# A hybrid transformer block on one core: sine tables in smaller steps, modulation columns in four steps, weight splits behind the squares at the first exit, and the latents' products two units abreast

## The chip, the core and the metric

The kernel runs on one core of a Trainium2 chip. The metric is the time of one execution on the device in microseconds (us). A core has a matrix engine (PE, with its weight loads, PEld, shown apart), three engines for elementwise work (DVE, ACT, POOL) and an engine that only issues DMAs here (SP). Each engine runs its instructions in the order in which the program queued them; an instruction that waits holds up all those behind it on its engine. POOL issues some of the DMAs too.

## The reference, cut to what matters

One layer, 512 tokens of width 1024, all in float32. The modulation vectors come from one vector `c`, each norm is followed by a scale and a shift, and two feed-forward networks stand around a mixer of two kinds of attention.

```python
mod = silu(c) @ w_ada + b_ada          # 9 x 1024: a shift, a scale and a gate for each part
sh1, s1, g1, sh2, s2, g2, sh3, s3, g3 = split(mod, 9)
h = rms(x) * (1 + s1) + sh1
x = x + 0.5 * g1 * swiglu(h, ffn1_w_in, ffn1_w_out)
h = rms(x) * (1 + s2) + sh2
x = x + g2 * mixer(h, cos(positions * freq), sin(positions * freq))   # gated delta rule and latent attention
h = rms(x) * (1 + s3) + sh3
x = x + 0.5 * g3 * swiglu(h, ffn2_w_in, ffn2_w_out)
```

The latent attention starts with low-rank products of `h` (384 columns of `w_in` for the queries, 256 for keys and values). Its rotary parts need the cosine and the sine of position times frequency.

## The kernel before, in words

**Layout and products.** `x` is held transposed: eight tiles `xT` of 128 features by 512 tokens. Every large product is done in three matmuls (`mm3`, L270 to 274, and its copy L899 to 901): each operand is split in a high part and a low rest (`wh`, `wl` of a weight tile `wr`; `hh`, `hl` of `h`; `ah`, `al` of the activations), and high x high, high x low and low x high are summed in PSUM (`pa`, `pb`). A weight unit is a tile of 1024 x 128 (or a part of it) that SP loads, ACT casts to `wh` and DVE subtracts to `wl`. In `split_w` (L202 to 206) there is another way for the low part: ACT negates the high part into `wl` (L205), and a DMA issued by POOL adds `wr` to it (L206). `plan_units` (L239) lists the units of the mixer and says which of them go that way; `prefetch` (L262) takes the next from the list.

**Stages.** `phase0` transposes and norms `x` and forms the first modulation vectors. `ffn1` runs the first feed-forward network: `enter1` (L903), then a grid of pairs in `ffn_pairs`, whose tasks have fixed steps, then `close` and `leave1` (L1113), which is called the first exit here. `mixer` begins with `latents` (L1320). After the mixer comes `ffn2`, with `leave2` at its end.

**The side work.** While the first feed-forward network keeps PE at work, a `Side` (L52) is advanced step by step; each step runs one generator to its next `yield`. Its generators are
- `ada` (L558): the modulation vectors of the later parts. For each of the 112 tiles of `w_ada` that they need, POOL issues a load (`ar`, L575) some tiles ahead, and DVE multiplies it by a column of silu(c) and adds it to `aa` (L584, L586). When the columns of a group are done, `ada_columns` (L599) sums `aa` over the partitions on PE (L605), copies the sum from PSUM on DVE (`rw`, L608), turns it by PE transposes (L612) and adds the bias on DVE (L616).
- `mixer_consts` (L1160): it loads the small constants of the mixer, transposes the convolution's weights (L1183, copy L1185), and forms angles, sines and cosines. `sincos` (L1253) is a row of small DVE passes on 128 x 128 tiles: a range reduction in two rounds (L1275) and two polynomials (L1285, L1291).

What a step of the side work queues stands, on each engine, between what the feed-forward queues before and after it. In the last pairs a step runs in three of seven program steps, and behind `stop` twice in each.

**A pair's activation.** In `pair_tasks` (L774) the gate's and up's products collect in PSUM (`pb`, L899 to 901); ACT copies a finished one to `cc` (L842), DVE adds (L851), ACT takes the SiLU (L852), DVE multiplies (L861), ACT and DVE split into `ah` and `al` (L863, L867), which the down products read (L272 to 274).

**The first exit.** The last six of the 22 feed-forward blocks of 128 are multiplied by `w_out` in units of their own (`unit_hi`, `unit_lo`, the `wl` of L1049). For the feature tiles 4 to 7, `leave1` does it in two halves of 256 tokens. After each tile DVE adds the product to `xT` (L975, `finish`), and `square_in` (L480) squares it on ACT (L488) and adds the square to `na`: for the first half on POOL (L490), else on DVE. `norm_half` (L492) then sums `na` over the partitions on PE (`colsum`, L548), turns the reciprocal root into a matrix `rb` that all partitions hold, and modulates: `hm` and `hl` on DVE, `hh` on ACT (L459 to 477). Of the weights of the first latents' units, one is asked for behind tile 4 and two behind tile 6 of the second half (`prefetch`).

**The latents.** `first_units` (L502) multiplies three units of `w_in` for the first half of tokens while that half's `h` is being made, then for the second half. `lead` units go abreast, feature tile by feature tile as `h` comes; the others follow one by one. The marks say after which of these steps the second half's norm goes on a step. A unit is asked for behind the first half, its ACT passes behind the last square.

Of the kernel before, what the change touches and what calls it, by code (L numbers as in the profile page):

```python
# [19 lines left out]
NT = 512  # L20
# [69 lines left out]
class Block:  # L90
# [148 lines left out]
    def plan_units(self):  # L239
# [10 lines left out]
        for c in (2056, 2184, 2312, 2440):  # L250
            cols(w, c, True)
# [10 lines left out]
    def prefetch(self, n):  # L262
        while len(self.ready) < n and self.specs:
            self.ready.append(self.specs.pop(0)())

# [193 lines left out]
    def modulate(self, kts, ts, rb, scale, shift, kept=None):  # L459
# [10 lines left out]
        for kt in kts:  # L470
# [3 lines left out]
            nc.scalar.activation(self.h[kt][0][:, ts], t, AF.Identity, bias=shift[:, kt:kt + 1])  # L474
# [5 lines left out]
    def square_in(self, t, ts, acc):  # L480
# [8 lines left out]
        eng = nc.gpsimd if w < NT and ts.start == 0 else nc.vector  # L489
# [12 lines left out]
    def first_units(self, n, nb, lead, marks):  # L502
# [11 lines left out]
        with self.matmuls_in_order(self.last_mm):  # L514
# [16 lines left out]
            with self.traced() as block:  # L531
                self.prefetch(1)
            for x in block:
                if x.engine == mybir.EngineType.Activation:
                    self.follow(x, self.squared)
# [63 lines left out]
    def ada_columns(self, c0, accs):  # L599
# [4 lines left out]
        for q, a in enumerate(accs):  # L604
            nc.tensor.matmul(pr[32 * q:32 * q + 32, :], self.ones[:, :32], a, start=True, stop=True,  # L605
                             tile_position=(0, 32 * q))
        rw = self.slot(s="rw")
        nc.vector.tensor_copy(rw[:32 * n, :], pr[:32 * n, :])  # L608
        yield
        pt = self.aux()  # L610
        for s in range(4):
            nc.tensor.transpose(pt[:, s * P:s * P + 32 * n], rw[:32 * n, s * P:(s + 1) * P], self.ident[:32 * n, :32 * n])  # L612
        col = self.const([P, 4 * n], s="mod")
# [28 lines left out]
    def ffn1(self):  # L642
# [6 lines left out]
        side.add(self.ada(((0, 1), (2, 3, 4, 5), (6, 7, 8, 9), (10, 11)), lambda i: 6 if i < 60 else 3, early=64), self.mixer_consts())  # L649
# [253 lines left out]
    def enter1(self, raws, split, products, glu, tick, side, w1):  # L903

        unit = lambda i: self.unit_split(raws, split, i)
        step = (side.step, 3)
# [20 lines left out]
    def ffn_pairs(self, w1, w2, gate, plain, raws, split, accs, side=None):  # L927
# [185 lines left out]
        def leave1():  # L1113
            accum = self.accum
            side.add(self.ada(((12, 13),), lambda i: 8))
            side.step()
            halves = [slice(0, HALF), slice(HALF, NT)]
            with self.matmuls_in_order(self.ends[mybir.EngineType.PE]):
                for half, ts in enumerate(halves):
                    for t in range(4, KT):  # L1120
# [5 lines left out]
                        self.square_in(t, ts, accum)  # L1126
                        if half and t in (4, 6):
                            self.prefetch(t // 2 - 1)
# [4 lines left out]
                self.prefetch(3)  # L1133
# [26 lines left out]
    def mixer_consts(self):  # L1160
# [19 lines left out]
        for _ in range(6):  # L1180
            yield
# [25 lines left out]
        for nm, gain, sc in (("q", self.gqr, 192.0 ** -0.5), ("k", self.gkr, 1.0)):  # L1207
            both = self.slot(s="rope").rearrange("p (e b c) -> p e b c", e=2, b=NB)
            c, s = both[:, 0], both[:, 1]
            for j in range(2):  # L1210
# [5 lines left out]
                                               op0=ALU.mult, op1=ALU.mult)  # L1216
            self.rope_c[nm], self.rope_s[nm] = c, s
# [35 lines left out]
    def sincos(self, ang):  # L1253
# [12 lines left out]
        for _ in range(2):  # L1266
# [7 lines left out]
            for src, c in ((kh, 0), (kl, 0), (kh, 1), (kl, 1), (kh, 2), (kl, 2), (kh, 3)):  # L1274
                v.scalar_tensor_tensor(out=r, in0=src, scalar=-cs[c], in1=r, op0=ALU.mult, op1=ALU.add)  # L1275
        yield
# [7 lines left out]
        for n in (11, 9, 7, 5, 3):  # L1284
            v.scalar_tensor_tensor(out=sn, in0=sn, scalar=(-1.0 if (n // 2) % 2 else 1.0) / f(n), in1=z, op0=ALU.add,  # L1285
                                   op1=ALU.mult)
# [952 lines left out]
```

## Time and profile before

| what | value |
|---|---|
| time, median of 3 runs | 1067.85 us (1066.84 to 1069.74) |
| time of the profiled execution | 1070.11 us |
| its span in the profile | 1068.4 us |
| mean granted clock of PE | 0.987 of full |
| busy: PE, PEld, DVE, ACT, POOL | 97%, 84%, 71%, 45%, 11% of the span |
| moved by DMA | 140.74 MB, 132 GB/s on the mean |

The stages as they lie in the span: the first feed-forward network to about 400 us with the first exit at its end, the latents from there on, the rest of the mixer and the second feed-forward network behind them.

How it is read: the profile gives busy times, and for each instruction what it waited for. A group or row reads engine, line, operation, output<-input by the program's names, shape. In rows in order of time, the start comes first, then the duration, and a wait ahead of it stands at the end in brackets with the work that ended it. In busy times by stretch, each stretch has its length, then PE, PEld, DVE, ACT and POOL with the number of instructions, then the clock granted to PE, then the DMA engines' share and GB/s. A matmul's duration overlaps that of the next one; the spacing of the starts tells what one costs.

### The profile page before, as it was taken

The page shows a single profiled execution, that of the slowest core. Times are in us where ns is not written, and L with a number is a line of the kernel's source. Part 1 is how long each engine was busy: PE and PEld are TensorE (multiplying, and loading weights), DVE is VectorE, ACT ScalarE, POOL GpSimd, SP SyncE. Part 2 cuts the span into 40 slices and gives each one's busy share as a digit, 9 for nine tenths or more (in the row PEclk, how much of TensorE's full clock was granted, in tenths as well). Part 3 has the DMA queues.
Part 4 walks back from the last instruction along what each step waited for, and adds up shares of the span by engine and source line. Part 5 has one row for each costly group of instructions (what it writes and reads, how often), then busy time and mean ns, then how long its engine had stood idle before and what let it go on. Part 6 is the DMA issues. An engine that isn't in the chain of part 4 may idle for free. (4 is left out here: it accounts for less than half of the span.)

```text
span 1068.4 us, 17063 instructions
## 1 busy us (share of the span) xinstructions
PE 1034.6 (97%) x6659; PEld 897.7 (84%) x6659; DVE 756.2 (71%) x1411; ACT 484.7 (45%) x865; POOL 117.6 (11%) x237
## 2 busy tenths in 40 slices
PE   6999999999999897999999999999999999999998
PEld 4787887888998786987877778988899999999997
DVE  4476888778785764857885765769767787777642
ACT  4342232255554252547747554465434444444332
POOL 0032222121101213100001021220000000000000
PEclk9999999999999997999999999999999999999999
DMA  9995876677664459622121211163432333233222
GB/s 272 280 279 173 273 237 207 191 206 191 177 168 110 124 133 231 159 60 54 48 78 35 77 34 40 41 130 90 137 99 80 119 119 98 81 119 99 65 75 79
DMA packets 187422, 140.74 MB, mean 132 GB/s; under 512 B 14401, under 2 KB 176206, under 8 KB 187342
## 3 DMA queue, kind: packets, MB, share of 16 engines
q1 hardware_dynamic: 175646, 100.33, 33.0%
q0 software_dynamic: 11696, 39.33, 13.5%
q8 instruction: 52, 0.85, 0.3%
q14 instruction: 28, 0.23, 0.1%
HBM read 127.18 MB, written 2.49 MB: 121 GB/s over the span
## 5 line engine op out<-in xcount | busy, mean ns | idle before, releaser
L272 PE MATMUL pa<-ah,wh 128*128 128x512 f32 (+1 forms) x346 | 134.6, 389 | 0.1
L273 PE MATMUL pa<-al,wh 128*128 128x512 f32 (+1 forms) x346 | 133.9, 387 | 0.0
L274 PE MATMUL pa<-ah,wl 128*128 128x512 f32 (+1 forms) x346 | 132.3, 382 | 0.5 <-DVE wl L1049 0.5
L272 PE MATMUL pa<-hh,wh 128*128 128x512 f32 (+1 forms) x293 | 110.7, 378 | 2.2 <-ACT hh L474 2.1
L273 PE MATMUL pa<-hl,wh 128*128 128x512 f32 (+1 forms) x293 | 109.8, 375 | 1.3 <-DVE hl L466 0.9
L274 PE MATMUL pa<-hh,wl 128*128 128x512 f32 (+1 forms) x293 | 108.7, 371 | 0.0
L575 POOL DMA_DIRECT2D ar<-in_w_ada x112 | 63.6, 589 | 174.9 <-DVE aa L586 60.8
L975 DVE SCALAR_TENSOR_TENSOR xT<-pa,mod,xT 128x512 f32<-128x512 f32 (+1 forms) x79 | 57.3, 728 | 35.0 <-PE pa L274 34.7
L274 PEld LDWEIGHTS pa<-ah,wl 128*128 128x128 f32 x346 | 66.1, 191 | 13.9 <-DVE wl L1049 0.9
L586 DVE SCALAR_TENSOR_TENSOR aa<-ar,sc,aa 128x512 f32<-128x512 f32 x98 | 73.2, 747 | 1.3
L272 PEld LDWEIGHTS pa<-ah,wh 128*128 128x128 f32 x346 | 66.9, 193 | 6.7 <-ACT ah L863 0.6
L273 PEld LDWEIGHTS pa<-al,wh 128*128 128x128 f32 x346 | 66.9, 193 | 5.9 <-DVE al L867 0.4
L272 PEld LDWEIGHTS pa<-hh,wh 128*128 128x128 f32 x293 | 55.5, 189 | 14.9 <-ACT hh L474 3.4
L899 PE MATMUL pb<-fh,wh 128*128 128x256 f32 x224 | 63.7, 285 | 0.9 <-ACT cc L842 0.8
L274 PEld LDWEIGHTS pa<-hh,wl 128*128 128x128 f32 x293 | 55.6, 190 | 10.5 <-issue 1.4
L273 PEld LDWEIGHTS pa<-hl,wh 128*128 128x128 f32 x293 | 55.5, 190 | 10.5 <-DVE hl L466 2.6
L901 PE MATMUL pb<-hh,wl 128*128 128x256 f32 x224 | 63.4, 283 | 0.0
L901 PE MATMUL pb<-fh,wl 128*128 128x256 f32 x224 | 63.3, 282 | 0.0
L900 PE MATMUL pb<-fl,wh 128*128 128x256 f32 x224 | 63.2, 282 | 0.0
L900 PE MATMUL pb<-hl,wh 128*128 128x256 f32 x224 | 63.2, 282 | 0.0
L899 PE MATMUL pb<-hh,wh 128*128 128x256 f32 x224 | 63.2, 282 | 0.0
L272 PE MATMUL pb<-hh,wh 128*128 128x512 f32 x149 | 58.6, 393 | 0.0
(448 smaller groups left out, 2789.4 us busy)
## 6 DMA issues: line engine op xcount, KB each, us to landing
wr<-in_ffn_w_in SPq DMA_DIRECT2D x82, 512.0 KB, 3.9
ar<-in_w_ada POOLq DMA_DIRECT2D x112, 256.0 KB, 4.8
wr<-in_ffn_w_out SPq DMA_DIRECT2D x32, 512.0 KB, 3.9
wr<-in_w_in SPq DMA_DIRECT2D x21, 512.0 KB, 3.9
wl<-wr POOLq DMA_DIRECT2D x19, 512.0 KB, 5.5
ar<-in_w_ada SPq DMA_DIRECT2D x16, 512.0 KB, 8.1
wr<-in_ffn_w_out SPq DMA_DIRECT2D x16, 384.0 KB, 3.7
wr<-in_w_out SPq DMA_DIRECT2D x8, 512.0 KB, 3.4
```

The lines of the kernel that those rows point to most:

```text
L272: mm(out, wh, xh, start=start, stop=False)
L273: mm(out, wh, xl, start=False, stop=False)
L274: mm(out, wl, xh, start=False, stop=stop)
L575: nc.gpsimd.dma_start(tiles[i], a1[kc * P:(kc + 1) * P, o:o + NT])
L586: nc.vector.scalar_tensor_tensor(out=acc, in0=a, scalar=sc, in1=acc, op0=ALU.mult, op1=ALU.add)
L899: mm(out, wh, xh, start=start and k == 0, stop=False, **kw)
L900: mm(out, wh, xl, start=False, stop=False, **kw)
L901: mm(out, wl, xh, start=False, stop=stop and k == 3, **kw)
L975: nc.vector.scalar_tensor_tensor(out=self.xT[t][:, ts], in0=p[:, ts], scalar=gate()[:, t:t + 1], in1=self.xT[t][:, ts], op0=ALU.mult, op1= ...
```

## The change

It has five parts; what the kernel computes stays as it was.

1. `ada_columns` yields in three more places, so the column sums, the copy, the transposes and the bias are queued in four steps. `enter1` advances the side work by four steps in place of three at each of its places; 68 of `ada`'s tiles in place of 64 come from the early pool.
2. `mixer_consts` yields four times in place of six ahead of the transpose of the convolution's weights, and within its loop over the rotary tables; `sincos` yields within its loops.
3. At the first exit the first half's squares are added on DVE (`pool=False`). The units' prefetch moves from the second half into the first: one unit behind tile 4, up to three behind tile 7, each with its ACT passes made to follow the last square so far (`prefetch_after`). The first unit gets its low part by a DVE subtraction, the others by ACT and DMA as before.
4. `first_units` runs two units abreast in place of one, and the unit asked for between the halves has its ACT passes behind the last `hh` of the modulation.
5. The last two column groups of `ada` (12 and 13) are started in `latents`, ahead of `first_units`, and not at the head of `leave1`.

```diff
-            cols(w, c, True)
+            cols(w, c, c > 2056)
...
+    def prefetch_after(self, n, name=None):
+        with self.traced() as block:
+            self.prefetch(n)
+        for x in block:
+            if x.engine == mybir.EngineType.Activation:
+                self.follow(x, name or self.squared)
...
-        eng = nc.gpsimd if w < NT and ts.start == 0 else nc.vector
+        eng = nc.gpsimd if pool and w < NT and ts.start == 0 else nc.vector
...
     def ada_columns(self, c0, accs):
...
+        yield
         rw = self.slot(s="rw")
         nc.vector.tensor_copy(rw[:32 * n, :], pr[:32 * n, :])
+        yield
         yield
         pt = self.aux()
...
+        yield
         col = self.const([P, 4 * n], s="mod")
...
-        step = (side.step, 3)
+        step = (side.step, 4)
...
         def leave1():
             accum = self.accum
-            side.add(self.ada(((12, 13),), lambda i: 8))
-            side.step()
...
-                        self.square_in(t, ts, accum)
-                        if half and t in (4, 6):
-                            self.prefetch(t // 2 - 1)
+                        self.square_in(t, ts, accum, False)
+                        if not half and t in (4, KT - 1):
+                            self.prefetch_after(1 if t == 4 else 3)
...
-                self.prefetch(3)
...
-        for _ in range(6):
+        for _ in range(4):
             yield
...
-            for src, c in ((kh, 0), (kl, 0), (kh, 1), (kl, 1), (kh, 2), (kl, 2), (kh, 3)):
+            for i, (src, c) in enumerate(((kh, 0), (kl, 0), (kh, 1), (kl, 1), (kh, 2), (kl, 2), (kh, 3))):
                 v.scalar_tensor_tensor(out=r, in0=src, scalar=-cs[c], in1=r, op0=ALU.mult, op1=ALU.add)
-        yield
+                if i in (2, 4, 6):
+                    yield
...
-        ps = self.first_units(3, nb, 1, (7, 15, 14))
+        self.side.add(self.ada(((12, 13),), lambda i: 8))
+        self.side.step()
+        ps = self.first_units(3, nb, 2, (7, 15, 14), self.modulated)
```

In the polynomials of `sincos` the yields stand after the terms 9 and 5 of the sine and 10, 6 and 2 of the cosine.

Three places show what moves. Lines are those of each kernel's own code (the changed one's run up to 16 lines higher), and the number behind a name tells tiles of one name apart.

On DVE, at the first column group (`aa` of the ada tiles, `rw` the copy of the sums, `mod` the finished columns), before:

```order
L772 TENSOR_TENSOR fl_937<-tv_918,fh_936 128x512
L989 TENSOR_TENSOR wl_859<-wr_857,wh_858 128x1024
L586 SCALAR_TENSOR_TENSOR aa_931<-ar_895,sc_124,aa_931 128x512
L586 SCALAR_TENSOR_TENSOR aa_931<-ar_898,sc_124,aa_931 128x512
L608 COPY rw_978<-pb_975 64x512
L586 SCALAR_TENSOR_TENSOR aa_931<-ar_901,sc_124,aa_931 128x512
L616 TENSOR_TENSOR mod_998<-pb_993,vT_126 128x4x2
```

The same place in the changed kernel:

```order
L590 SCALAR_TENSOR_TENSOR aa_906<-ar_863,sc_124,aa_906 128x512
L613 COPY rw_950<-pb_919 64x512
L590 SCALAR_TENSOR_TENSOR aa_906<-ar_866,sc_124,aa_906 128x512
L694 TENSOR_TENSOR wl_934<-wr_826,wh_933 128x1024
L590 SCALAR_TENSOR_TENSOR aa_906<-ar_908,sc_124,aa_906 128x512
L779 TENSOR_TENSOR fl_957<-tv_937,fh_956 128x512
L996 TENSOR_TENSOR wl_871<-wr_869,wh_870 128x1024
L590 SCALAR_TENSOR_TENSOR aa_906<-ar_911,sc_124,aa_906 128x512
L623 TENSOR_TENSOR mod_985<-pb_969,vT_126 128x4x2
```

The copy of the sums has moved ahead of `fl` and `wl`, and three products lie between it and the bias, where there was one.

On DVE, near the end of the sine block (`sr`, `sz`, `sk`, `skl` are its tiles, `uc` a pair's sum for the SiLU, `wl` a weight's low part), before:

```order
L1275 SCALAR_TENSOR_TENSOR sr_3508<-skh_3512,sr_3508 128x128
L1049 TENSOR_TENSOR wl_3522<-wr_3347,wh_3521 128x768
L1278 TENSOR_SCALAR sr_3508<-sr_3508 128x128
L1279 TENSOR_TENSOR sz_3583<-sr_3508 128x128
L1283 TENSOR_SCALAR sk_3510<-sz_3583 128x128
L1285 SCALAR_TENSOR_TENSOR sk_3510<-sk_3510,sz_3583 128x128 x5
L1287 SCALAR_TENSOR_TENSOR sk_3510<-sk_3510,sr_3508 128x128
L851 TENSOR_TENSOR uc_3305<-uc_3305,pb_3202 128x256
```

In the changed kernel:

```order
L1056 TENSOR_TENSOR wl_3534<-wr_3362,wh_3533 128x768
L1280 SCALAR_TENSOR_TENSOR sr_3468<-skl_3471,sr_3468 128x128
L1280 SCALAR_TENSOR_TENSOR sr_3468<-skh_3472,sr_3468 128x128
L1284 TENSOR_SCALAR sr_3468<-sr_3468 128x128
L1285 TENSOR_TENSOR sz_3583<-sr_3468 128x128
L858 TENSOR_TENSOR uc_3320<-uc_3320,pb_3215 128x256
L1289 TENSOR_SCALAR sk_3470<-sz_3583 128x128
L1291 SCALAR_TENSOR_TENSOR sk_3470<-sk_3470,sz_3583 128x128 x4
```

The pair's sum now stands ahead of the sine's polynomial and not behind it, and the weight's low part stands within the reduction.

On ACT, at the first exit (`sq` the squares, `wh` and `wl` the splits of the latents' units, `rb` the norm's spread), before:

```order
L488 ACTIVATE sq_3782<-xT_106 128x512
L488 ACTIVATE sq_3786<-xT_106 128x512
L203 CAST wh_3936<-wr_3935 128x1024
L205 ACTIVATE wl_3937<-wr_3935 128x1024
L203 CAST wh_4009<-wr_4008 128x1024
L205 ACTIVATE wl_4010<-wr_4008 128x1024
L203 CAST wh_4062<-wr_4061 128x1024
L205 ACTIVATE wl_4063<-wr_4061 128x1024
L488 ACTIVATE sq_3825<-xT_106 128x256
L488 ACTIVATE sq_3848<-xT_106 128x256
L488 ACTIVATE sq_3871<-xT_106 128x256
L488 ACTIVATE sq_3894<-xT_106 128x256
```

In the changed kernel:

```order
L496 ACTIVATE sq_3782<-xT_106 128x512
L496 ACTIVATE sq_3786<-xT_106 128x512
L496 ACTIVATE sq_3809<-xT_106 128x256
L203 CAST wh_3813<-wr_3812 128x1024
L496 ACTIVATE sq_3838<-xT_106 128x256
L496 ACTIVATE sq_3861<-xT_106 128x256
L496 ACTIVATE sq_3884<-xT_106 128x256
L203 CAST wh_3888<-wr_3887 128x1024
L205 ACTIVATE wl_3889<-wr_3887 128x1024
L203 CAST wh_3895<-wr_3894 128x1024
L205 ACTIVATE wl_3896<-wr_3894 128x1024
```

Of six passes that stood ahead of the four squares of the first half, one cast now stands among them and four behind them.

More of the change, by code (lines that the diff above doesn't have):

```diff
@@ L473, in modulate @@
                                            op0=ALU.mult, op1=ALU.mult)
-            nc.scalar.activation(self.h[kt][0][:, ts], t, AF.Identity, bias=shift[:, kt:kt + 1])
+            self.modulated = nc.scalar.activation(self.h[kt][0][:, ts], t, AF.Identity, bias=shift[:, kt:kt + 1]).ins.name
             if last:
@@ L478, in modulate, with square_in @@
         low(*last)
-    def square_in(self, t, ts, acc):
+    def square_in(self, t, ts, acc, pool=True):
         nc = self.nc
@@ L500, in norm_half, with first_units @@
             yield
-    def first_units(self, n, nb, lead, marks):
+    def first_units(self, n, nb, lead, marks, before=None):
         units = [self.next_unit(ahead=0) for _ in range(n)]
@@ L530, in first_units @@
             drain(nb)
[L531 to L535, printed above, removed]
+            self.prefetch_after(1, before)
             ts = slice(HALF, NT)
@@ L648, in ffn1 @@
         side = self.side = Side()
-        side.add(self.ada(((0, 1), (2, 3, 4, 5), (6, 7, 8, 9), (10, 11)), lambda i: 6 if i < 60 else 3, early=64), self.mixer_consts())
+        side.add(self.ada(((0, 1), (2, 3, 4, 5), (6, 7, 8, 9), (10, 11)), lambda i: 6 if i < 60 else 3, early=68), self.mixer_consts())
         def tail():
@@ L1273, in sincos @@
             yield
-            for src, c in ((kh, 0), (kl, 0), (kh, 1), (kl, 1), (kh, 2), (kl, 2), (kh, 3)):
+            for i, (src, c) in enumerate(((kh, 0), (kl, 0), (kh, 1), (kl, 1), (kh, 2), (kl, 2), (kh, 3))):
                 v.scalar_tensor_tensor(out=r, in0=src, scalar=-cs[c], in1=r, op0=ALU.mult, op1=ALU.add)
-        yield
+                if i in (2, 4, 6):
+                    yield
         z = self.slot(s="sz")[:, :P]
@@ L1286, in sincos @@
                                    op1=ALU.mult)
+            if n in (9, 5):
+                yield
         v.scalar_tensor_tensor(out=sn, in0=sn, scalar=1.0, in1=r, op0=ALU.add, op1=ALU.mult)
@@ L1292, in sincos @@
                                    op1=ALU.mult)
+            if n in (10, 6, 2):
+                yield
         v.tensor_scalar(out=cn, in0=cn, scalar1=1.0, scalar2=None, op0=ALU.add)
```

## The prediction

> **What bounds the kernel now.** I read the page first, then the list of who waited for whom with PE as the waiter, then the busy times by stretch, and last the instructions in order of time around each wait.
>
> ```profile
> span 1068.4 us, 17063 instructions
> PE 1034.6 (97%) x6659; PEld 897.7 (84%) x6659; DVE 756.2 (71%) x1411; ACT 484.7 (45%) x865; POOL 117.6 (11%) x237
> ```
>
> PE holds the time: all others have room, so an edit counts only where it changes how PE stands or runs. PE's own waits are few:
>
> ```profile
> PE pb L548 <- POOL na L490: 4.5, 1, 4.5
> PE pb L899 <- ACT cc L842: 4.1, 2, 3.3
> PE pb L612 <- DVE rw L608: 1.8, 1, 1.8
> PE pa L274 <- DVE wl L1049: 0.5, 1, 0.5
> ```
>
> The columns are the sum, the times and the longest. The waits are only half of the loss. The next rows (stretch, length, PE busy, then PEld, DVE, ACT, POOL, then the granted clock) lie on a grid of 3.4 us, on which the clock was seen to change:
>
> ```profile
> 105.50:108.90 3.40, 1.62 (x10) 1.20 (x10) 3.33 (x7) 0.00 (x0) 1.41 (x3) 1.00 0.96 310
> 108.90:112.30 3.40, 3.40 (x10) 2.63 (x9) 3.37 (x6) 1.33 (x2) 0.94 (x2) 0.50 1.09 364
> 371.80:375.20 3.40, 2.88 (x13) 2.88 (x14) 3.12 (x14) 0.47 (x2) 0.54 (x1) 0.50 0.63 177
> 375.20:378.60 3.40, 3.40 (x9) 1.94 (x8) 3.31 (x9) 1.54 (x3) 0.55 (x1) 0.51 0.49 142
> 412.70:416.10 3.40, 2.37 (x16) 1.90 (x14) 3.40 (x10) 2.53 (x6) 0.00 (x0) 1.00 1.00 326
> 416.10:419.50 3.40, 1.91 (x8) 0.97 (x6) 2.38 (x6) 2.39 (x6) 0.91 (x1) 1.00 0.85 279
> 419.50:422.90 3.40, 3.30 (x14) 3.07 (x15) 1.05 (x3) 0.45 (x2) 0.41 (x1) 0.50 0.77 148
> ```
>
> A stretch with 1.62 or 1.91 of PE work is followed by one at half clock; one with 2.37 is not. A half-clock stretch in which PE works loses 1.7. So each wait of PE is paid about twice.
>
> **A: the columns at 107 us.** PE in order of time, then DVE:
>
> ```profile
> 97.51 0.39 PE L272 MATMUL pb<-hh,wh 128*128 128x512 f32 x1
> 103.04 1.05 PE L605 MATMUL pb<-aa,ones 128*32 128x512 f32 x4
> 104.02 0.50 PE L272 MATMUL pb<-hh,wh 128*128 128x512 f32 x1
> 107.46 0.46 PE L612 MATMUL pb<-ident,rw 64*128 64x64 f32 x4 [1.78 <-DVE rw L608]
> ```
> ```profile
> 97.78 0.69 DVE L695 TENSOR_TENSOR af<-sg,pa 128x512 f32<-128x512 f32 x1 [7.35 <-PE pa L274]
> 100.69 0.75 DVE L586 SCALAR_TENSOR_TENSOR aa<-ar,sc,aa 128x512 f32<-128x512 f32 x1
> 106.73 0.68 DVE L608 COPY rw<-pb 64x512 f32<-64x512 f32 x1
> ```
>
> The transposes (L612) wait for the copy of the sums, which DVE reaches at 106.73 behind other work. Now the sums stand 24 matmuls earlier, at 97.5; they take 104.02 - 103.04 = 1.0, twelve matmuls follow at (103.04 - 97.51)/24 = 0.23, so PE is at the transposes at 97.5 + 1.0 + 2.8 = 101.3. The copy stands right behind the product of 100.69 and ends at 100.69 + 0.65 + 0.68 = 102.0. A wait of 0.8 is left: 1.0 saved. That stretch then holds 3.4 - 0.8 = 2.6 of PE work, above 2.37, so I let its half clock go too: 1.7. A = 2.7; bounds 0 (the copy as late as now) and 1.78 + 1.7 = 3.5. The five products that four steps instead of three pull ahead are 5 x 0.65 = 3.3 on DVE, which idles 7.35 before 97.78; without that cover they would cost those 3.3. Each also issues its load on POOL's queue earlier, where nothing else waits then. The other three column groups have no wait of PE before and keep the copy several products ahead of the transposes: nothing.
>
> The Trainium skill speaks against the second half of this term: "TensorE: Matmul & The Clock Gate" (Part 1, What's actually happening, and Why this matters for your kernels) has the clock halved after a whole idle window of some 3.4 us and warns of gaps of over some 3 us, so by it a gap of 1.78 costs no clock and A would be 1.0. The row 108.90:112.30 shows half clock right behind that gap, so the trace does not agree, and it decides.
>
> **B: the sine tables, 351 to 386 us.** DVE, ACT and PE:
>
> ```profile
> 351.63 0.41 DVE L861 TENSOR_TENSOR cc<-cc,uc 128x256 f32<-128x256 f32 x1
> 354.10 0.69 DVE L867 TENSOR_TENSOR al<-cc,ah 128x512 fp32r<-128x512 f32 x1
> 356.51 0.22 DVE L1185 COPY cwT<-pb 128x57 f32<-128x57 f32 x1 [1.73 <-PE pb L1183]
> 380.67 0.42 DVE L851 TENSOR_TENSOR uc<-uc,pb 128x256 f32<-128x256 f32 x1 [1.94 <-PE pb L901]
> 383.18 0.69 DVE L867 TENSOR_TENSOR al<-cc,ah 128x512 fp32r<-128x512 f32 x1
> ```
> ```profile
> 370.86 0.42 ACT L852 ACTIVATE uc<-uc 128x256 f32<-128x256 f32 x1 [11.62 <-DVE uc L851]
> ```
> ```profile
> 350.42 0.28 PE L899 MATMUL pb<-hh,wh 128*128 128x256 f32 x1
> 385.49 0.39 PE L273 MATMUL pa<-al,wh 128*128 128x512 f32 x1
> 412.83 0.28 PE L274 MATMUL pb<-ah,wl 128*128 128x256 f32 x1
> 412.95 0.28 PE L272 MATMUL pa<-hh,wh 128*128 128x256 f32 x1
> ```
>
> ACT stands 11.62 us at one SiLU because DVE's L851 lies behind the sine block; the PSUM copy that frees PE's next product (cc L842) stands behind it, so PE waits 3.3 and then runs 371.80 to 378.60 at half clock. Now two iteration steps fewer (four instead of six) bring L1183 right behind the product that starts at 350.42 (12 matmuls, started 412.95 - 412.83 = 0.12 apart at full clock, so 351.85; DVE's copy 352.15), and L851 stands between the steps. DVE has no less to do: from 356.51 to the last al, 383.87, are 27.4, less its one long wait 25.4; in front of the block's start it no longer has the six rows from 351.63 to 354.10, 3.1 with the last one, and does them in between. So al ends at 352.15 + 25.4 + 3.1 = 380.6. PE by itself would reach its reader (the row at 385.49) 6.9 earlier (3.3 + 0.5 of waits, 3.1 of half clock), at 378.6; it waits for al, and gets there 385.49 - 380.65 = 4.8 earlier. DVE is late next. B = 4.8; bounds 3.3 (only the wait) and 6.9.
>
> **C: the first exit, 400 to 430 us.** PE, ACT and DVE:
>
> ```profile
> 404.47 1.01 PE L548 MATMUL pb<-ones,na 128*128 128x1 f32 x4 [4.46 <-POOL na L490]
> 430.22 0.28 PE L272 MATMUL pa<-hh,wh 128*128 128x256 f32 x1
> ```
> ```profile
> 393.25 1.03 ACT L203 CAST wh<-wr 128x1024 fp32r<-128x1024 f32 x1
> 398.93 1.64 ACT L488 ACTIVATE sq<-xT 128x256 f32<-128x256 f32 x5
> ```
> ```profile
> 396.81 0.48 DVE L975 SCALAR_TENSOR_TENSOR xT<-pb,mod,xT 128x256 f32<-128x256 f32 x1 [1.57 <-PE pb L274]
> 431.09 0.48 DVE L466 SCALAR_TENSOR_TENSOR hl<-hm,mod,hh 128x256 fp32r<-128x256 f32 x1
> 431.49 0.48 DVE L472 SCALAR_TENSOR_TENSOR hm<-xT,mod,rb 128x256 f32<-128x256 f32 x1
> ```
>
> From the wait's start (404.47 - 4.46 = 400.0) to the second half's first matmul (430.22) are 30.2. In it lie 45 matmuls of the down products and 72 of the latents' first half, at 0.12 each 14.0, and two column sums and two spreads: half of 1.01, and two steps of 0.12, each twice: 1.5. At full clock 15.5: 14.7 are lost to waits and half clock.
>
> What is left of them afterwards: (1) The sum's wait. The squares stood behind six ACT passes (393.25 to 398.93) and were added on POOL. Now one cast stands among them and DVE adds. The last tile is done at 397.3; 1.64/5 = 0.33 for its square, 0.42 for the add (as long as the 128x256 sum at 351.63) and hand-overs 0.2 make 398.3, 1.7 ahead of PE. Of that B takes 1.5, as DVE gains 3.3 there (383.87 to 380.6) and PE 4.8, and DVE's subtraction of the first unit, which a DMA did, takes 1.1, partly in DVE's idle 1.57: I leave 0.3. (2) The first half with two units abreast: 48 matmuls, a sum, a spread are 6.5 on PE. DVE has 16 passes at 0.40 (431.09 to 431.49), a third kind of pass 0.4, two adds 0.7, and two hand-overs of some 0.4: 8.3. It starts about 1.0 ahead, and 1.7 of PE's work follow its last pass: 8.3 - 1.0 + 1.7 = 9.0, 2.5 lost. The splits that stood between ACT's hh passes come behind them now; the DMAs that finish them have over 5 us until their units are due. C = 14.7 - 0.3 - 2.5 = 11.9; bounds 4.5 (only the sum's wait) and 14.7.
>
> The moved loads of the last columns (ada 12, 13) leave PE alone: behind the exit, DVE uses them after its modulation, bar the last hl (rival 3). The second exit keeps its order. Sum: 2.7 + 4.8 + 11.9 = 19.4. The profiled execution took 1070.11, its span 1068.4 and 1.7 around it: 1050.7. The median of the three runs is 2.26 lower, 1067.85: 1048.4.
>
> **Rivals.**
>
> 1. Half clock comes back at the exit. In (2) PE waits 2.5 in 9, about half of it in one stretch; by the rows above 1.9 of work in 3.4 is too little and 2.4 enough, and I get 2.1 to 2.5. One or two stretches: 1.7 or 3.4 more, 1050 to 1052. For it: 419.50. Against: PE's gaps are halved.
> 2. The clock does not follow short gaps. Then A keeps its 1.7, and C the half clock behind the row 416.10:419.50, two stretches less PE's wait, 2.5: 1048.4 + 4.2 = 1052.6. This is what the Trainium skill's page "TensorE: Matmul & The Clock Gate" (Part 1, What's actually happening) says of gaps shorter than its window. Against it: half clock follows both thin stretches and not the one between.
> 3. The late loads. DVE's first product of them stands before the last hl of the second half.
>
> ```profile
> ar<-in_w_ada POOLq DMA_DIRECT2D x112, 256.0 KB, 4.8
> ar<-in_w_ada SPq DMA_DIRECT2D x16, 512.0 KB, 8.1
> ```
>
> POOL issues them at about 411, PE needs that hl at about 413 + 7 x 9 x 0.12 = 420.5. At 4.8 they are in, at 8.1 barely; beyond 9.5 each us is one of PE, and half clock with it. At 12: 2.5 + 1.7, 1052.6.
> 4. Slower: the four steps pull loads forward between 56 and 98 us, into the feed-forward's own loads.
>
> ```profile
> wr<-in_ffn_w_in SPq DMA_DIRECT2D x82, 512.0 KB, 3.9
> ```
>
> If the five weight tiles of that time land in 8.1 instead of 3.9 and nothing covers it, PE waits 5 x 4.2 = 21, and a half-clock stretch at each, 8.5: 1048.4 + 29.5 = 1077.9. It turns slower when over 19.4 of this is uncovered. Against: PE has no wait between 20 and 105 us, and DVE idles 7.35.
>
> **How the numbers follow.** Forecast 0.55, rival 1 0.22, rival 2 0.11, rival 3 0.08, rival 4 0.04. The likeliest gives 1048.4. Low end: A and B at their upper bounds add 0.8 + 2.1, C without its 0.3 and a little of the 2.5 another 1: 1044.5. High end: rivals 1 to 3 to 1052.6, and B and A at their lower bounds (1.5 + 2.7) with rival 1's 3.4: 1056. About 0.3% (3.2 us) is what a measurement of this kernel can tell from no change. Faster by more: all but rival 4 and a rest, 0.95; within 0.02; slower 0.03.
>
> **What would show it.** In the changed profile: L612's wait under 1 with full clock at 109 to 112; no wait on cc of over 1 near 368, but one of about 1.5 on ah or al near 380; L548 without a wait on na; the second half of the latents starting some 17 to 19 us earlier, at 411 to 414, and everything behind it as much earlier. Wrong would be: half clock again at 406 to 413 (rival 1); a wait on hl near 420 behind aa (rival 3); waits on wh or wl before 100 (rival 4); DVE's al at 384 as before (B gone).

## The result and the profile after

The changed kernel takes 1057.12 us (median of four runs, 1053.83 to 1061.71) against 1068.56: a ratio of 0.9897, interval 0.9857 to 0.9937. It is faster, but by 11.4 where 19.4 were forecast, and 1.1 above the range. The profiled execution is the fastest of the four, 1053.83, so the two profiles differ by 16.3. Where these lie comes first; why the other executions gain less comes with the experiments.

The page's first lines, and the rows of PE's list of waits on which the reading rests:

```profile
span 1052.1 us, 17065 instructions
PE 1025.9 (98%) x6659; PEld 891.2 (85%) x6659; DVE 757.8 (72%) x1416; ACT 484.9 (46%) x864; POOL 114.4 (11%) x232
```
```profile
PE pb L552 <- DVE lsq L1350: 1.7, 1, 1.7
PE pa L281 <- DVE al L874: 1.2, 1, 1.2
PE pb L906 <- ACT cc L849: 1.1, 1, 1.1
PE pa L280 <- ACT lsq L1346: 0.7, 1, 0.7
PE pb L618 <- DVE rw L613: 0.5, 1, 0.5
```

Three waits of before are as forecast: the 4.5 on `na` is gone, the 3.3 on `cc` at 372 us is gone (the 1.1 of the list stands at 211.6 us, where before had 0.8), and on `rw` 0.5 is left of 1.8. At 369.8 us there is a wait of 1.2 on `al` instead. The two on `lsq` are new and were in no sum: `lsq` are the squares of the latents, formed behind the first units' products. (A third new one, 0.8 on a weight's low part at 220 us, is part of the -0.7 in the table below; its cause is not shown.) The stretches on the 3.41 us grid of this execution, on which its clock changes (at 430.60 and 434.01), at the places that answer to those of before (the first two rows hold the transposes, now at 101.1, and what is behind them):

```profile
99.51:102.92 3.41, 2.94 (x16) 2.11 (x15) 3.41 (x6) 2.52 (x3) 1.07 (x2) 1.00 0.38 124
102.92:106.33 3.41, 3.41 (x17) 2.81 (x16) 3.38 (x7) 0.00 (x0) 0.63 (x2) 1.00 0.88 277
365.74:369.16 3.42, 2.70 (x14) 1.78 (x13) 3.21 (x12) 1.74 (x3) 0.00 (x0) 1.00 0.40 117
396.46:399.88 3.42, 2.83 (x22) 2.42 (x21) 3.24 (x9) 2.44 (x6) 0.00 (x0) 1.00 0.96 168
427.18:430.60 3.42, 1.74 (x13) 1.24 (x11) 2.95 (x5) 1.01 (x2) 0.00 (x0) 1.00 1.11 330
430.60:434.01 3.41, 3.41 (x11) 2.73 (x11) 2.92 (x5) 0.00 (x0) 1.49 (x1) 0.50 1.21 290
```

The clock is full at all three places of the forecast, and there is a new thin stretch (1.74 of PE work) with half clock behind it, at 427 to 434.

The starts of the same matmul in both traces show how far PE is ahead of the kernel before at each place:

| PE's matmul, before | after | ahead | the stretch ending here |
|---|---|---|---|
| 90.03 | 89.09 | 0.94 | start of the program |
| 112.28 | 108.47 | 3.81 | first columns: +2.9 |
| 358.18 | 355.11 | 3.07 | -0.7 |
| 380.47 | 371.75 | 8.72 | sine tables: +5.7 |
| 430.22 | 409.18 | 21.04 | first exit: +12.3 |
| 455.03 | 438.53 | 16.50 | latents: -4.5 |
| 1039.99 | 1023.67 | 16.32 | -0.2 |

So up to the second half of the latents all that was forecast is there (2.9, 5.7 and 12.3 for 2.7, 4.8 and 11.9), and then 4.5 is given back within 30 us. The new waits in order of time, DVE and PE:

```profile
411.63 0.48 DVE L474 SCALAR_TENSOR_TENSOR hl<-hm,mod,hh 128x256 fp32r<-128x256 f32 x1
415.49 0.48 DVE L588 TENSOR_SCALAR aa<-ar,sc 128x512 f32<-128x512 f32 x1 [3.38 <-DMA ar<-in_w_ada]
415.89 0.48 DVE L474 SCALAR_TENSOR_TENSOR hl<-hm,mod,hh 128x256 fp32r<-128x256 f32 x1
416.28 5.47 DVE L590 SCALAR_TENSOR_TENSOR aa<-ar,sc,aa 128x512 f32<-128x512 f32 x7
429.05 0.68 DVE L1350 TENSOR_TENSOR lsq<-lsq,lsq 128x512 f32<-128x512 f32 x1
```
```profile
424.17 0.50 PE L280 MATMUL pa<-hh,wh 128*128 128x512 f32 x1 [0.72 <-ACT lsq L1346]
429.79 1.16 PE L552 MATMUL pb<-ones,lsq 128*128 128x1 f32 x8 [1.68 <-DVE lsq L1350]
```

DVE stands 3.38 at the first product of the moved column groups, whose tile of `w_ada` has not landed, and `hl`, seven more products and the latents' splits are queued behind it. `hl` is in time for PE; the squares are 0.72 and 1.68 late, and half clock follows.

How long these tiles take from issue to landing, first the eight that the kernel before asks for at the head of its first exit (issued from 365 to 375 us), then the first seven of the changed kernel (406.6 to 410.6 us):

```profile
DMA to landing us min/median/max: 3.0/3.4/5.3
DMA to landing us min/median/max: 8.6/9.0/9.3
```

### The profile page after: what moved, and what is told of

Read it like the earlier page. It is cut to its first block, busy times and chain, and to the rows that moved or that the text cites. A ratio compares the mean times of both kernels' runs of the same rounds, so it can differ in the third digit from the quotient of the medians.

```text
span 1052.1 us, 17065 instructions
## 1 busy us (share of the span) xinstructions
PE 1025.9 (98%) x6659; PEld 891.2 (85%) x6659; DVE 757.8 (72%) x1416; ACT 484.9 (46%) x864; POOL 114.4 (11%) x232
## 5 line engine op out<-in xcount | busy, mean ns | idle before, releaser
L282 PEld LDWEIGHTS pa<-hh,wl 128*128 128x128 f32 x293 | 55.7, 190 | 10.6 <-issue 1.5
```

Of the source, the lines that this page charges most:

```text
L282: mm(out, wl, xh, start=False, stop=stop)
```

## The experiments

All ratios are to the kernel before on the same chip, with their interval. "Ahead" is PE's lead over the kernel before, as in the table above, in the profiled run; the start of the program alone makes between 0 and 1.1 of it (in e14 it is 1.9 behind).

| run | median us | ratio | ahead at 112 | 380 | 430 | 455 | 1040 |
|---|---|---|---|---|---|---|---|
| e0 changed again | 1058.85 | 0.9909 (0.9896 to 0.9923) | 3.5 | 8.7 | 21.1 | 11.8 | 11.7 |
| e1 loads back | 1052.39 | 0.9853 (0.9839 to 0.9867) | 3.3 | 8.2 | 16.3 | 16.3 | 17.7 |
| e2 columns undone | 1055.81 | 0.9891 (0.9875 to 0.9906) | 2.0 | 6.1 | 17.7 | 14.8 | 16.7 |
| e3 sines undone | 1062.05 | 0.9947 (0.9934 to 0.9961) | 3.4 | -0.4 | 11.9 | 8.0 | 7.3 |
| e4 loads at exit's end | 1057.14 | 0.9890 (0.9869 to 0.9912) | 3.3 | 8.6 | 20.9 | 16.5 | 17.9 |
| e5 as e4, no columns | 1051.43 | 0.9849 (0.9836 to 0.9862) | 0.3 | 5.2 | 16.2 | 16.1 | 17.4 |
| e6 as e4, adds on POOL | 1054.85 | 0.9881 (0.9862 to 0.9901) | 3.7 | 8.8 | 20.5 | 12.1 | 11.9 |
| e7 as e4, one abreast | 1052.61 | 0.9868 (0.9853 to 0.9883) | 3.6 | 9.0 | 17.6 | 17.6 | 19.0 |
| e8 without the 16 loads | 1049.44 | 0.9833 (0.9817 to 0.9849) | 3.6 | 8.7 | 21.0 | 21.0 | 20.9 |
| e9 as e8, no columns | 1052.71 | 0.9857 (0.9840 to 0.9873) | 0.2 | 5.2 | 16.2 | 16.2 | 17.4 |
| e10 as e8, late units | 1047.33 | 0.9819 (0.9798 to 0.9839) | 4.0 | 9.6 | 21.9 | 21.9 | 23.5 |
| e11 columns in the mixer | 1050.02 | 0.9845 (0.9822 to 0.9868) | 3.7 | 8.5 | 20.8 | 20.8 | 20.4 |
| e12 as e11, late units | 1050.70 | 0.9830 (0.9817 to 0.9844) | 3.4 | 8.2 | 20.5 | 20.5 | 19.8 |
| e13 late units, loads at head | 1051.01 | 0.9831 (0.9818 to 0.9845) | 3.6 | 8.9 | 17.8 | 17.8 | 19.4 |
| e14 as e8, no sines | 1058.23 | 0.9901 (0.9888 to 0.9915) | 0.9 | -3.0 | 9.3 | 9.4 | 10.6 |
| e15 as e8, one abreast | 1052.38 | 0.9846 (0.9833 to 0.9860) | 3.6 | 9.3 | 17.5 | 17.5 | 19.0 |

The column of 430 against that of 455 tells most of it. A kernel that is 20 or more ahead at 430 and starts all loads of groups 12 and 13 in the latents, or just ahead of them (e4, e6), loses 4 to 9 by 455. One that has no such loads there, or starts them at the exit and is at 17.8 or less, loses nothing. e2 and e3, with the loads where the change put them, lose 3 to 4 from 17.7 and 11.9: at that place a lead of 12 is enough for a late tile, on which DVE waits 1.4 in e2 and 2.4 in e3. So the place of the loads counts. The lead counts too: e5 has the loads where e4 has them, is 4.7 less ahead and loses nothing. (e7 is no such pair with e4; POOL issues its loads 8 us earlier.)

### e0: the changed kernel again

> The changed kernel once more, for the spread of its runs. Theory: the spread (1053.8 to 1061.7 in four runs) is half clock that falls in some runs and not in others, as the 3.41 us grid lies differently against the waits of PE that are left; then the median is 1055 to 1059 and a run's time follows its mean granted clock, 0.001 of clock for about 1.05 us. Rival: the spread comes from transfers; then runs of one clock differ by several us.

Four runs within 0.9 us at 1058.85, all at a clock of 0.995. Its late squares are later still. PE, and ACT ahead of it:

```profile
433.50 1.87 PE L552 MATMUL pb<-ones,lsq 128*128 128x1 f32 x8 [4.96 <-DVE lsq L1350]
```
```profile
430.54 1.04 ACT L203 CAST wh<-wr 128x1024 fp32r<-128x1024 f32 x1 [3.62 <-DMA wr<-in_w_in]
431.49 0.59 ACT L1346 ACTIVATE lsq<-pa 128x512 f32<-128x512 f32 x1
```

Besides the tile of `w_ada` there is now a weight tile of the latents themselves that lands late: ACT waits 3.62 for it with the square queued behind. Neither expectation holds alone: half clock is part of the spread, but the wait it follows differs by 3.3 from one execution to the next, and that is a transfer.

### e1: the loads back at the exit's head

```diff
+            side.add(self.ada(((12, 13),), lambda i: 8))
+            side.step()
             halves = [slice(0, HALF), slice(HALF, NT)]
...
-        self.side.add(self.ada(((12, 13),), lambda i: 8))
-        self.side.step()
         ps = self.first_units(3, nb, 2, (7, 15, 14), self.modulated)
```

> The changed kernel with the last two column groups (ada 12, 13) started at the head of the first exit again. Theory: their late loads cost the changed kernel 4.6 us in the profiled run (DVE stands 3.4 for the first tile, the eight products and the latents' splits come that much later, PE waits 0.7 and 1.7 for the squares and then runs a stretch at half clock), so this one is 4 to 5 us faster than the changed kernel, 1052 to 1053, with no wait of DVE on a tile of w_ada and no wait of PE over 0.5 on the latents' squares. Rival: it is the units' splits, which now stand behind the modulation on ACT, that make the squares late; then this one is like the changed kernel, 1057, with the wait of 1.7 still there.

1052.39, 6.5 faster than e0: no wait of DVE on `ar`, none of PE on `lsq`, nothing lost after 430. But it is only 16.3 ahead there. With the loads at the head, the squares' adds stand on DVE behind a tile of the second half (390.76), which waits for PE, and PE then waits for them at the norm's sum:

```profile
390.76 0.48 DVE L982 SCALAR_TENSOR_TENSOR xT<-pa,mod,xT 128x256 f32<-128x256 f32 x1 [1.68 <-PE pa L282]
391.16 0.42 DVE L498 TENSOR_TENSOR na<-na,sq 128x256 f32<-128x256 f32 x1
391.49 1.22 DVE L208 TENSOR_TENSOR wl<-wr,wh 128x1024 fp32r<-128x1024 f32 x1
392.63 1.47 DVE L498 TENSOR_TENSOR na<-na,sq 128x256 f32<-128x256 f32 x3
```

```profile
PE pb L552 <- DVE na L498: 2.4, 1, 2.4
```

A stretch of half clock follows at 394.5. Taking the move back thus costs 4.2 at the exit and saves 4.5 to 9.3 behind it. The theory of the late loads holds. That the move changes nothing at the exit does not: 4.2 of the 12.3 gained there hang on it.

### e4 to e7: the loads at the exit's end, and parts of the exit

```diff
                 drain(na)
+            side.add(self.ada(((12, 13),), lambda i: 8))
+            side.step()
             return self.norm_half(1, accum, 3)
```

The two lines are taken out of `latents`, as in e1.

> The changed kernel with the last two column groups started at the end of the first exit, so that POOL issues their loads ahead of one unit's low part and not behind it. Theory: the order at the exit stays the changed kernel's (second half of the latents about 21 us ahead of the kernel before), and the loads, some 4 us earlier, are in when DVE asks: no wait on a tile of w_ada, no late squares. Then 1048 to 1050. Rival 1: the unit's low part, now behind eight loads on POOL's queue, comes late in place of the loads: a wait of PE on a weight's DMA of 1 to 3 us, 1051 to 1053. Rival 2: moving the loads ahead puts the squares' order out again, as at the exit's head (a wait of 2.4 on the norm's sum): 1052.

The loads now land in time, DVE has no wait on them, and PE still waits 2.0 for `lsq`, because ACT waits for a weight tile:

```profile
426.78 1.05 ACT L203 CAST wh<-wr 128x1024 fp32r<-128x1024 f32 x1 [3.09 <-DMA wr<-in_w_in]
427.73 0.59 ACT L1346 ACTIVATE lsq<-pa 128x512 f32<-128x512 f32 x1
```

Six runs from 1051.63 to 1058.99. The theory that only the order on POOL's queue is at fault falls: asked for some 4 us earlier, the loads are in time, and then something else is late, a tile that SP loads. That suggests that the transfers together are what is short; e8 takes them out.

e5 is e4 with the columns' steps of before:

> The kernel with the loads at the exit's end, with the modulation columns in the former steps. With the late loads gone, what the columns are worth shows alone. Theory A: their wait of 1.3 and a half-clock stretch of 1.7 in every run: 3 slower than the kernel with the loads at the exit's end. Theory B: the half clock behind that wait depends on how the 3.41 us grid lies against it and falls in some runs only: 1.3 to 3 slower, with runs that differ by 1.7. Rival: the columns' steps cost as much elsewhere as they save: no difference.

1051.43, faster by 5.7: being 4.7 later at 430, it loses nothing behind it. It says nothing on the columns' worth; e9 does.

e6 puts the adds back on POOL (`square_in(t, ts, accum)`), e7 runs one unit abreast (`first_units(3, nb, 1, ...)`):

> The kernel with the loads at the exit's end, with the first half's squares added on POOL again. Theory: it was the ACT passes ahead of the squares and the DMA issues between the adds that made the sum late; with these gone four adds of 0.7 to 1.0 on POOL end at most 1.5 after those on DVE: 0 to 1.5 slower, with full clock. Rival: the adds on POOL are the cost: 3 to 5 slower, a wait of PE on POOL's na of 3 or more and half clock behind it.

> The kernel with the loads at the exit's end, with the latents' first half one unit abreast again. Theory: the first half takes 17.3 again in place of 11.8, since DVE sets the pace of the first unit, PE works less than 2 in a grid stretch and two stretches run at half clock: 4 to 5.5 slower. Rival: only the half clock comes from elsewhere and the waits are as before: 2 to 2.5 slower at full clock.

From 380 to 430, e6 gains 11.7 where e4 gains 12.3, so with the other edits in, adds on POOL cost 0.6 and do not make the sum late. Behind 430 it loses 8.3, with ACT standing 5.5 for a weight tile. e7 gains 8.6 for 12.3, with two stretches of half clock, as its theory has it; its total is nonetheless better than e4's, as e5's is.

### e8: the transfers taken out

In `ada`, the tiles of groups 12 and 13 are not loaded; the products are formed from a tile of `x`, so the last gate is not the reference's (in e9, e10, e14 and e15 likewise). DVE does the same passes.

```diff
                 _, c, kc = steps[i]
+                if c >= 12:
+                    tiles[i], loaded = self.xT[0], i + 1
+                    continue
                 tiles[i] = tile(i, "ar")
```

> The changed kernel without the 16 loads of the last two column groups (4.2 MB): their products are formed from x, so the last gate is not the reference's; DVE does the same passes. Theory: with PE some 21 us ahead, the transfers between the exit and the latents no longer fit: the DMA engines are at a share of 1.0 from 395 to 435 us, and a weight tile of the latents lands up to 5 late, in some runs more than in others. Without these loads nothing is late: the gain of 21 at the second half stays to the end, 1047 to 1049, and the runs lie within 2 us. Rival: the tile is late because its load is issued late, when its buffer comes free (414.7), whatever else is moved: then a wait on it stays, 1053 to 1058.

1049.44 (four runs, 1049.03 to 1051.91), and all 21.0 of the lead stay. The last two columns of the next rows are the DMA engines' share and GB/s. Before:

```profile
395.00:405.00 10.00, 5.54 (x45) 5.34 (x44) 2.64 (x4) 5.57 (x10) 5.89 (x8) 0.87 0.68 129
405.00:415.00 10.00, 9.30 (x57) 8.85 (x56) 5.43 (x15) 2.99 (x8) 0.72 (x1) 0.79 1.03 266
415.00:425.00 10.00, 8.07 (x35) 6.83 (x36) 5.09 (x14) 3.94 (x8) 3.41 (x6) 0.73 0.72 190
425.00:435.00 10.00, 10.00 (x78) 9.88 (x78) 7.84 (x19) 4.24 (x9) 1.45 (x3) 0.93 0.56 197
```

The changed kernel:

```profile
395.00:405.00 10.00, 8.85 (x65) 8.00 (x64) 9.04 (x24) 6.03 (x13) 1.07 (x2) 1.00 0.96 217
405.00:415.00 10.00, 10.00 (x84) 9.95 (x84) 6.03 (x15) 4.91 (x10) 4.71 (x9) 1.00 1.05 325
415.00:425.00 10.00, 9.28 (x53) 7.84 (x53) 8.16 (x12) 4.92 (x7) 5.72 (x10) 1.00 1.06 361
425.00:435.00 10.00, 8.32 (x34) 6.59 (x33) 7.96 (x12) 3.95 (x6) 1.49 (x1) 0.83 1.13 291
```

The kernel without the 16 loads:

```profile
405.00:415.00 10.00, 10.00 (x85) 9.95 (x84) 8.81 (x20) 4.94 (x10) 0.89 (x1) 1.00 0.93 253
415.00:425.00 10.00, 10.00 (x58) 8.77 (x57) 8.06 (x12) 7.27 (x10) 0.85 (x1) 1.00 0.67 158
425.00:435.00 10.00, 10.00 (x50) 8.35 (x49) 9.15 (x15) 4.16 (x7) 1.48 (x1) 1.00 0.76 200
```

Before, these 40 us moved 7.8 MB (the sum of the last column by 10 us); in the changed kernel they move 11.9. Of the 4.1 more, 2.1 are eight of the 16 loads, which in the kernel before were in by 378 us: part 5 of the change brought them here, not PE's lead. The rest comes with the earlier stage: the last two of the 16, which landed at 448 and 449 before, and what else now falls into the stretch. The share of the DMA engines is no measure of the room that is left (1.03 before at 266 GB/s, 1.06 now at 361); the times to landing are, 8.6 to 9.3 where 3.0 to 5.3 were. Without the 16 x 256 KB no engine waits for a transfer here. So the 16 loads are the cause, and the rival, a weight tile that is late because it is asked for late, is out.

The sum of bytes alone does not decide it. e5 and e7 move 11.7 MB in the same 40 us (e5: 189, 333, 353 and 296 GB/s by 10 us), and nothing is late in them; they are 4.7 and 3.3 us later than e4. What is missing is a few us, not a large part of the transfers.

### e9, e14, e15: the terms by themselves, with nothing late behind them

Each is e8 with one part as it was in the kernel before: the columns (with three side steps and 64 early tiles), the sine block and the six steps ahead of it, one unit abreast.

> The kernel without the 16 loads, with the modulation columns in the former steps. Theory: with nothing late behind, the columns' worth shows: their wait, 1.3, and a stretch of half clock of 1.7 in the runs in which the grid lies so: 1.3 to 3 slower than the kernel without the loads. Rival: the columns give nothing in the end: within 0.5.

3.3 slower, and of the lead at 112 it lacks 2.7 (0.2 gained there for 2.9): the columns are worth about what was forecast. Their wait of 1.8 is back and half clock is behind it in the profiled run:

```profile
105.70:109.11 3.41, 1.63 (x10) 1.37 (x10) 3.34 (x8) 0.00 (x0) 1.24 (x3) 1.00 0.96 322
109.11:112.53 3.42, 3.42 (x9) 2.65 (x8) 3.38 (x6) 1.53 (x3) 1.07 (x2) 0.50 1.06 356
```

> The kernel without the 16 loads, with the sine block in its former large steps. Theory: as in the complete kernel with these steps, the stretch of the sines ends 9.2 later (a wait of 5.5 on the copied product, 2.6 on a weight's low part, ten us of half clock), and nothing hides it now: 1058 to 1059. Rival: what was measured in the kernel before, 5.7: 1055.

8.8 slower: PE has a whole grid stretch without work, the first of three at half clock.

```profile
PE pb L909 <- ACT cc L852: 6.6, 2, 5.5
PE pa L282 <- DVE wl L1059: 2.6, 1, 2.6
```

That is more than the 5.7 of the step from before to changed, as in e3: with the other edits in, the undivided block stands worse than it did in the kernel before (a wait of 5.5 for 3.3). What a part gains when added and what it costs when undone are two numbers here.

> The kernel without the 16 loads, with the latents' first half one unit abreast. Theory: the second half of the latents starts 3.7 later, as in the complete kernel, and nothing hides it: 1053. Rival: the units' passes on ACT between the halves make up for it: within 1 of 1049.4.

2.9 slower, 4.2 of PE's lead at 430; a thin stretch and half clock, as in the kernel before:

```profile
397.90:401.31 3.41, 1.90 (x9) 1.31 (x10) 3.23 (x10) 2.12 (x5) 0.00 (x0) 1.00 0.88 202
401.31:404.73 3.42, 3.28 (x14) 2.58 (x13) 2.05 (x5) 2.62 (x4) 0.00 (x0) 0.51 0.94 282
404.73:408.14 3.41, 3.41 (x17) 3.41 (x18) 0.71 (x3) 0.18 (x1) 1.54 (x2) 0.50 1.07 355
```

### e2 and e3: undoing a part in the complete kernel

> The changed kernel with the modulation columns in the former steps (no further yields, three side steps at the first stage, 64 early tiles). Theory: the wait of 1.8 on the copied sums near 106 comes back and half clock behind it, 2.9 together: 1060 against the changed kernel's 1057. Rival (clock does not follow so short a gap): only the wait, 1.3 more, 1058.4, with full clock behind it.

> The changed kernel with the sine block in its former large steps (and the six steps ahead of it). Theory: the wait of 3.3 on the copied product and the half clock behind it come back, 5.7 in the profiled run: 1062.8, and up to 1.5 more if DVE, later by some 3, is late at the norm's sum too. Rival: the sine steps gave only the wait, 3.3: 1060.4, with half clock behind 372 found in the changed kernel too.

e2 came out 3.0 faster than e0, against both expectations: its lead at 430 is 17.7, and it loses 2.8 behind it where e0 loses 9.3. (Its four executions spread from 1053.8 to 1059.0 and the changed kernel's eight from 1053.8 to 1061.7, so faster is not shown, only that the loss of 2.9 is not seen.) e3 is 3.2 slower than e0; it is 9.2 later at 380 than the changed kernel, and against e0 it gets more than half of that back, as it loses 3.9 behind 430 and e0 9.3. In a kernel with a shortage ahead, undoing a gain can cost little; e9 and e14 undo the same parts without the loads. e2 has one thing more to show. It has the wait of 1.8 too, but at full clock:

```profile
105.60:109.01 3.41, 1.99 (x11) 1.66 (x12) 3.35 (x7) 0.00 (x0) 1.23 (x3) 1.00 0.97 318
109.01:112.43 3.42, 3.42 (x17) 2.84 (x16) 3.38 (x6) 1.90 (x3) 1.11 (x3) 1.00 1.07 361
```

Here the grid cuts the wait so that 1.99 of work is left in the stretch, against 1.63 in e9. Undoing the columns cost 1.3 at that place in e2 (1.6 gained for 2.9), and 2.7 to 2.8 in e5 and e9.

### e10 and e13: what mended the sum at the exit

e10 is e8 with the units asked for in the second half, as before (`if half and t in (4, 6): self.prefetch(t // 2 - 1)`, and `self.prefetch(3)` behind it). e13 is the changed kernel with that and with the loads at the head as in e1.

> The kernel without the 16 loads, with the units asked for in the exit's second half again, as in the kernel before (adds on DVE, two abreast, as changed). Theory: the ACT passes of these units stand among the squares again, the norm's sum comes 3 to 4.5 late and half clock follows: 5 to 8 slower than the kernel without the loads. Rival: the adds on DVE alone had mended the sum: at most 2 slower, full clock at the exit.

> The changed kernel with two edits of the exit undone together: the units asked for in the second half, and the loads of the last column groups at the exit's head (the adds stay on DVE, two abreast). Theory: only these two together put all five split passes of ACT ahead of the first half's squares, and that was the late sum: a wait of 3 to 4.5 on the norm's sum and half clock behind it, second half of the latents 6 to 9 later than in the changed kernel; nothing is late behind that, 1053 to 1057. Rival: the adds on POOL between DMA issues were the late sum: no wait over 1.5 on it, second half at the changed kernel's place.

e10 is no slower at the exit (12.3): the theory that the new place of the units alone mends the sum falls. In e13 ACT's five passes stand ahead of the squares, as expected:

```profile
384.99 2.93 ACT L203 CAST wh<-wr 128x1024 fp32r<-128x1024 f32 x3
387.83 2.00 ACT L205 ACTIVATE wl<-wr 128x1024 fp32r<-128x1024 f32 x2
389.74 1.63 ACT L496 ACTIVATE sq<-xT 128x256 f32<-128x256 f32 x5
```

PE then waits 1.6 for the sum, with one stretch of half clock: 3.4 lost at the exit, half of what was expected. In e1 and in e10, with one of the two edits each, the five passes do not all stand ahead of the squares; so for ACT either the units' earlier place or the removed loads suffices. How much of the 3.4 is ACT's is not shown: in e13 too the adds stand on DVE behind a tile of the second half (390.08) that waits 1.56 for PE, and e1 loses 4.2 with such an order on DVE and without those passes in the way.

### e11 and e12: complete kernels without the shortage

e11 starts the last two column groups in the mixer's second group of units, where transfers are few:

```diff
-        self.side.add(self.ada(((12, 13),), lambda i: 8))
-        self.side.step()
...
+        deltas.add(self.ada(((12, 13),), lambda i: 4))
+        deltas.step()
         chain.add(self.delta_k(kT), self.delta_a(kT), bases())
-        self.dense_units(4, Rates(sides, (0.75, 0, 1.5)), 1, conv_done(0, qT))
+        self.dense_units(4, Rates(sides, (0.75, 0.75, 1.5)), 1, conv_done(0, qT))
```

> The changed kernel with the last two column groups (loads, products, sums) moved out of the latents into the mixer's second group of four units; all is computed. Theory: as without the loads, the transfers fit, and DVE has eight products less in front of the latents' squares: 1047 to 1050, runs within 2 us. Rival: DVE and the transfers are short there too, and PE waits for the convolutions: 1052 or more, with new waits of PE between 490 and 520.

> The kernel with the last column groups in the mixer, with the units asked for in the exit's second half as in the kernel before; all is computed. Theory: asking later costs nothing at the exit and takes transfers out of it, as in the kernel without loads (2 faster there): 1047 to 1049. Rival: the 2 there were the spread of half clock: as with the columns in the mixer alone, 1050.

1050.02 and 1050.70: both beat the two kernels given, by some 18 and 6 to 9 us, and are near to the kernel that leaves the loads out (one execution of e11's four took 1055.36). In the mixer these loads land 2.9 to 3.6 us after their issue. From 455 to 1040 the lead falls by 0.4 and 0.7, where e1 and e4 gain 1.4: PE has new waits of 1.7 and 1.5 on DVE there, at 612 and 649 us, later than the rival has them and not at the convolutions. The late units add nothing. Of the 2.6 that e10 is further ahead at 1040 than e8, 0.9 are there by 380, ahead of the edit, and 1.7 are a half-clock stretch behind the mixer that e8 has and e10 has not, as some other executions have it and others not.

## Why the prediction was wrong

- **A, the columns (2.7 forecast):** 2.9 in the profile, 3.3 by e9. The mechanism was right: the wait is 0.5 where 0.8 was worked out, the transposes start at 101.1, or 102.0 without the 0.9 of lead from the start of the program, where 101.3 + 0.8 = 102.1 was worked out, and the clock behind them is full. That the clock part is not there in every execution (e2) was in the bounds.
- **B, the sine tables (4.8):** 5.7. PE did wait for an `al`, as forecast, but 1.2, and for the `al` of an earlier reader than was worked out. The one that the forecast named ends at 375.9 (379.0 with the lead of 3.1 from ahead of the block added, for 380.6) and is read at 376.8 without a wait, so DVE was not as late as its sum had it.
- **C, the exit (11.9):** 12.3: 18.05 from where the wait stood (391.13) to the second half, where 15.5 + 0.3 + 2.5 = 18.3 were worked out. Rival 1, half clock at the exit, did not come: 2.83 of work in the thinnest stretch, for 2.1 to 2.5 worked out. The size was right, but the cause given for the first part was too simple, and in that the agreement is partly luck: the splits ahead of the squares were cleared by more than one edit, the adds on POOL counted 0.6, and 4.2 of the 12.3 hang on the moved loads (e1), to which the forecast gave no part in it.
- **The step that failed** is "The moved loads of the last columns (ada 12, 13) leave PE alone". It was a term of 0, with the load held against a time to land of 4.8 or 8.1 from the page of before. The first seven took 8.6 to 9.3, in a stretch into which part 5 itself had put eight of the 16 loads and which PE reaches 20 us earlier; what they do to the other transfers was not asked. The term measures -4.5 in the profiled execution and -9.3 in e0, and e8 puts it at 7.7 to 9.4 by the medians (1049.44 against 1057.12 and 1058.85). The forecast without it, 1048.4, lies 1.0 from what e8 takes. The step beside it, on the DMAs that finish the low parts of the latents' weights, held: PE has no wait on one there in the changed kernel, and 0.3 and 1.0 in e4 and e6.
- **Rival 3** named the late loads, at 0.08 and for 1052.6, by way of the last `hl`. `hl` was in time. The late tile acted through the queue behind it on DVE, and in e0 a weight tile that no rival named acted through ACT.
- **Rival 2**, a clock that does not follow short gaps, is out: e9 has half clock behind a wait of 1.8. That it follows each of them is out as well (e2). Rival 4 is out: PE waited for no weight tile between 20 and 100 us.
- The forecast and the table of leads go by one profiled execution each. In the changed kernel that execution is the best of four, so the profile shows less of the loss than the median has; e0's shows more.

## What to carry to other kernels

When an edit moves loads into a stretch, and other edits pull the engine that bounds it forward, add up what that stretch must now move before asking of each load whether it lands in time; here 7.8 MB in 40 us became 11.9. Such a rise is a rival to be given a chance, not yet a verdict: 11.7 MB did no harm in kernels whose PE came 3 to 5 us later. A time to land that is taken from a page of before holds for the traffic of before. A part that is undone in a kernel with a shortage further on seems worth little or less than nothing; take the shortage out first (here, 16 loads) and measure the parts then. Work that nobody needs soon, as the last gate's columns, belongs where transfers are few, not where its code happens to fit.

## What the runs showed of the clock

Over the 18 traces, on the grid of 3.41 us and from 25 to 1035 us: of stretches at full clock, all 16 with under 1.75 of PE work were followed by one at half clock, of 21 with 1.77 to 2.07 eight were, and of those with 2.08 or more a single one, with 2.46 (e2, at 430 to 433 us, behind a wait of 1.0). At half clock PE came back to full behind every stretch that it worked through (3.41), and behind none of the 11 with a gap, not even with 3.31. So in these traces a wait of 1.4 to 2 costs its own length or 1.7 more, and a small gap soon after it another 1.7. How the grid cuts the wait explains most of it; between 1.77 and 2.07 of work, and for the one at 2.46, what decides is not shown. The Trainium skill ("TensorE: Matmul & The Clock Gate", What's actually happening) asks for a whole idle window of about 3.4 us for the lower clock; these traces do not agree, a window half idle is enough.
